# Seam between two layers: the post-norm's second product and both sums of squares move to GpSimd

## The chip, the cores and the metric

The kernel runs on one core of one Trainium2 chip. The metric is the device time of one execution in microseconds (us). A core has a matrix engine (TensorE, PE in the profile; its weight loads are PEld), a vector engine (VectorE, DVE), an activation engine (ScalarE, ACT), a programmable vector engine (GpSimd, POOL) and a sequencer that only issues transfers here (SyncE, SP). Each engine runs its own instructions strictly in their written order; semaphores make an instruction wait for one on another engine. SBUF is the on-chip working memory of 128 partitions, PSUM the small memory into which TensorE writes.

## The reference

Two equal layers (`DEPTH = 2`) on `x` of 512 tokens by 1024 features, float32. Each layer normalises `x`, makes one wide projection, runs a gated linear recurrence (8 heads) and a sliding-window attention (16 heads) on parts of it, gates both, and projects back:

```python
def rms_norm(x, g):
    y = xf * lax.rsqrt(jnp.mean(xf * xf, axis=-1, keepdims=True) + NORM_EPS)
    return (y * g.astype(jnp.float32)).astype(x.dtype)

def hybrid_layer(x, w_in, w_out, g_pre, g_post, lb, g_head, sinks):
    h = rms_norm(x, g_pre)
    proj = jnp.einsum('bsd,de->bse', h, w_in)
    ...
    y = jnp.einsum('bse,ed->bsd', jnp.concatenate([o_h, o_a], axis=-1), w_out)
    return x + rms_norm(y, g_post)
```

What matters here is the end of one layer and the start of the next: `x + rms_norm(y, g_post)`, then `rms_norm(., g_pre)` of the next layer, on 1024 features per token.

## The kernel before

**Tiles.** The 512 tokens are four tiles of 128 (`tt` 0 to 3, one token per partition). The 1024 features of a tile are two halves of 512 (`ch` or `c`, 0 and 1), since one PSUM bank holds 128x512 float32. Every matrix product is float32 made of three products of a high and a low part; weights and activations are split into `whi`/`wlo` and `hhi`/`hlo` by a cast on ScalarE (L178, L401) and a subtraction on VectorE (L179, L405).

**The stream of matrix products.** All projections of both layers stand in one queue of units. A unit accumulates one 128x512 (or 128x256) result in one of three PSUM banks `pj` (L284) and has an evacuation that runs when it is done. The last units of layer 0 are the eight of the out projection's last part (four tiles by two halves); the next are the key and value units of layer 1 (`wkv`, four tiles, 128x256), which need the new normalised and transposed activations `hhi`, `hlo` tile by tile; after them come the query units of layer 1, which need all four tiles.

**The seam.** For each tile, `final` and `pre_norm` do this, in this order of dependence:

- L850 (VectorE): adds the unit's result out of PSUM to `y`, per half.
- L892 (ScalarE): square of the half of `y`, with the row's sum into a column of `ss`.
- L894 (GpSimd): `y` of half 0 times the post-norm's weight `gpost`, in place. L899 (VectorE): the same for half 1, into `yg` (shown as tile `s`).
- `rstd2`: L343 (VectorE) adds the two sums of squares and epsilon, one number per row; L345 (GpSimd) raises it to the power -1/2: `r`.
- L906 (VectorE), per half: `x` plus the product times `r`, which is the layer's output (tile `a`); a transfer stores it.
- `pre_norm`: L377 (ScalarE) squares each half of `a` with its sum, `rstd2` again (L343, L345), L392 (VectorE) scales each half with the row's factor and the next weight, which lies in PSUM (`xn`).
- `rest`: L397 (TensorE) transposes four blocks of a half of `xn` into one of three PSUM banks `sc`, L401 (ScalarE) makes `hhi`, L405 (VectorE) `hlo` of it.

**What sets the order.** The code is written in the order of the stream of units; a scheduler then orders each engine's instructions by that order and by when it reckons their inputs ready, except where `pin` keeps the written order (the transposes L397 are pinned). So the order of the seam's instructions on VectorE and ScalarE depends on the engines that the program names.

Of the kernel before, what the change touches and what calls it, by code (L numbers as in the profile page):

```python
# [10 lines left out]
F32 = mybir.dt.float32  # L11
# [3 lines left out]
ALU = mybir.AluOpType  # L15
# [10 lines left out]
EPS = 1e-6  # L26
# [43 lines left out]
def hybrid_kernel(ctx: ExitStack, tc: tile.TileContext, x, wkv, win, wout, g_pre, g_post, lbp, ghead, sinks,  # L70
                  gcol_c, cos_f, sin_f, cos_t, sin_t, masks_c, out):
    nc = tc.nc
    P = 128
# [5 lines left out]
    sm = ctx.enter_context(tc.tile_pool(name="sm", bufs=4))  # L79
# [16 lines left out]
    def ac():  # L96
        return ps.tile([P, 512], F32, tag="ac", name="ac", bufs=8 - PJ - SC)

    def tmp(tag, dt=F32, n=1):

        t = tp.tile([P, n, 512] if n > 1 else [P, 512], dt, tag=tag, name=tag, bufs=TB[tag])
        return t
# [96 lines left out]
    def later(steps, key, fn):  # L199

        waiting.append([steps, key, fn])
# [138 lines left out]
    def rstd2(ss, keep=lambda ins: ins):  # L340

        t = sm.tile([P, 1], F32, tag="s1", name="s1")
        keep(nc.vector.scalar_tensor_tensor(t, ss[:, 0:1], EPS, ss[:, 1:2], op0=ALU.add, op1=ALU.add))  # L343
        r = sm.tile([P, 1], F32, tag="r1", name="r1")
        keep(nc.gpsimd.tensor_tensor(r, t, mhalf[:, 0:1], op=ALU.pow))  # L345
        return r

    def halves(tag):
        t = tmp(tag, n=2)
        return [t[:, 0], t[:, 1]]  # L350

    def load_g(g):
        t = halves("b")
        for c in range(2):
            nc.sync.dma_start(t[c], g[c * 512:(c + 1) * 512].partition_broadcast(P))
        return t
# [57 lines left out]
    def pre_norm(tt, xt, g, hT, key, defer):  # L414
        m = Norm(tt, xt, g, hT)
        m.square(0)
        m.square(1)
        m.r = rstd2(m.ss)
        m.scale(0)
        m.scale(1)  # L420
        later(defer, None, lambda: m.rest(0))
        later(defer, key, lambda: m.rest(1))

    def new_hT():
        return (hp.tile([P, KT, SEQ], F32R, tag="hhi", name="hhi"), hp.tile([P, KT, SEQ], F32R, tag="hlo", name="hlo"))


    def layer(l, last):
# [243 lines left out]
        def hgrn(a):  # L672
# [3 lines left out]
            for j, f, k, q, A in hs:  # L676
                f2, k2, q2 = (blocks(t, 2) for t in (f, k, q))
                qb, kb = halves("b")
                qb2, kb2 = blocks(qb, 2), blocks(kb, 2)
                re = halves("a")[0][:, 0:256]  # L680
                nc.vector.reciprocal(re, f2[:, :, 1])  # L681
                nc.scalar.copy(qb2[:, :, 0], q2[:, :, 0])
                nc.vector.tensor_tensor(qb2[:, :, 1], q2[:, :, 1], f2[:, :, 1], op=ALU.mult)
                nc.scalar.copy(kb2[:, :, 0], k2[:, :, 0])
                nc.vector.tensor_tensor(kb2[:, :, 1], k2[:, :, 1], re, op=ALU.mult)
                qbs.append(qb)
                kbs.append(kb)

                nc.gpsimd.tensor_tensor(k2[:, :, 0], k2[:, :, 0], f2[:, :, 1], op=ALU.mult)
                nc.vector.tensor_tensor(q2, qb2, f2[:, :, 0].unsqueeze(2).broadcast_to([P, SEQ // 2, 2]), op=ALU.mult)  # L690
                nc.vector.tensor_tensor(f2[:, :, 0], f2[:, :, 0], f2[:, :, 1], op=ALU.mult)
                tots.append(f2[:, :, 0])
                yield 3.5
# [174 lines left out]
        hT2 = {}  # L868

        def final(tt, ch, c0, n):  # L870
            split = n < 512
            if ch == 0:
                if tt == 0:
                    hT2["gpost"] = load_g(g_post[l])
                    if not last:
                        hT2["gpre"] = [ac() for _ in range(2)]
                        for c, t in enumerate(load_g(g_pre[l + 1])):
                            nc.scalar.copy(hT2["gpre"][c], t)
                        state["limit"] = slab_first["in", l + 1, QA][0] + 2
                        hT[l + 1] = new_hT()  # L880
                hT2["x"] = halves("a")
                for c in range(2):
                    nc.sync.dma_start(hT2["x"][c], (x if l == 0 else x_mid)[tt * P:(tt + 1) * P, c * 512:(c + 1) * 512])
                hT2["ss"] = sm.tile([P, 2], F32, tag="ss", name="ss")
            xt, ss, y = hT2["x"], hT2["ss"], yt[tt]
            if c0:

                hT2["ss"] = sm.tile([P, 2], F32, tag="ss", name="ss")
                nc.vector.tensor_tensor(hT2["ss"][:, 0:1], ss[:, 0:1], ss[:, 1:2], op=ALU.add)
                ss = hT2["ss"]  # L890
            junk = tmp("u")
            nc.scalar.activation(junk[:, 0:n], y[:, ch, c0:c0 + n], AF.Square, scale=1.0 / 32.0, accum_out=ss[:, ch:ch + 1])  # L892
            if ch == 0:
                nc.gpsimd.tensor_tensor(y[:, 0], y[:, 0], hT2["gpost"][0], op=ALU.mult)  # L894
                return
            if not c0:
                hT2["yg"] = tmp("s")
            yg = hT2["yg"]
            nc.vector.tensor_tensor(yg[:, c0:c0 + n], y[:, 1, c0:c0 + n], hT2["gpost"][1][:, c0:c0 + n], op=ALU.mult)  # L899
            if split and not c0:  # L900
                return
            r = rstd2(ss)
            parts = [(0, y[:, 0], 0, 512)] + [(1, yg, e, n) for e in range(0, 512, n)]
            for i, (c, v, e, w) in enumerate(parts):
                xs = xt[c][:, e:e + w]
                nc.vector.scalar_tensor_tensor(xs, v[:, e:e + w], r, xs, op0=ALU.mult, op1=ALU.add)  # L906
                (nc.scalar if split and i == 1 else nc.sync).dma_start(
                    (out if last else x_mid)[tt * P:(tt + 1) * P, c * 512 + e:c * 512 + e + w], xs)
            if not last:
                pre_norm(tt, xt, hT2["gpre"], hT[l + 1], ("h", l + 1, tt), DEFER)  # L910
# [48 lines left out]
    mhalf = const.tile([P, 4], F32, name="mhalf")  # L959
# [23 lines left out]
    m, n = head[0], head[1]  # L983
# [146 lines left out]
```

## Time and profile before

| | |
|---|---|
| median of 3 runs (lowest, highest) | 927.55 us (927.0, 927.8) |
| the profiled execution: its time, its span | 927.92 us, 926.2 us |
| granted TensorE clock, mean | 0.999 |
| busy: PE, DVE, ACT, POOL | 908.4, 672.1, 462.5, 268.8 us |
| the seam, from the first L894 to the first query unit of layer 1 | 444.7 to 480.65 us of the span |

A row of a timeline gives the start in us from the span's beginning, the duration in us, the engine, the line, the operation, output<-inputs by the program's names, the shape, and in brackets the idle time of the engine before it and what ended it. Consecutive alike instructions are merged (x2, x8). A row of a group by tile gives minimum, median and maximum in ns, then first and last start. A row of waits gives the total in us, how often, and the longest. A row of windows gives the length and the busy time of each engine, with the instructions counted, in that stretch.

### The profile page before, as it was taken

The numbers are of one execution on the slowest core, as the hardware profiler recorded it, in microseconds if no ns is written. First come the engines' busy times: TensorE is split into PE (matmuls) and PEld (weight loads), VectorE is DVE, ScalarE is ACT, GpSimd is POOL, SyncE is SP. The second block draws the span as 40 slices with busy tenths as digits, with TensorE's granted clock in tenths as the row PEclk, the third lists the DMA queues.
The fourth block names the chain that finished last, engine by engine and source line by source line (L and its number), as shares of the span: only waits on it lengthen the run. The fifth ranks groups of instructions, "written<-read, shape, count | busy, mean of one in ns | idle before, by whom it ended". The sixth has DMA issues, their size and how long they took to land.

```text
span 926.2 us, 18985 instructions
## 1 busy us (share of the span) xinstructions
PE 908.4 (98%) x7240; PEld 751.1 (81%) x7240; DVE 672.1 (73%) x1326; ACT 462.5 (50%) x1100; POOL 268.8 (29%) x286
## 2 busy tenths in 40 slices
PE   8999999999999999999989999999999999999996
PEld 6888887878888888788878878888787887888885
DVE  5968977885766783955786689878867577748556
ACT  5535767536364451444453466674554636325242
POOL 3425443242221311311332254441323203113102
PEclk9999999999999999999999999999999999999999
DMA  6684612322222242423356555122223223323213
GB/s 223 187 234 135 171 36 80 92 82 80 70 86 94 64 136 69 138 70 112 117 160 178 162 148 171 58 69 92 70 80 99 62 81 114 104 70 94 91 35 136
DMA packets 56570, 100.74 MB, mean 109 GB/s; under 512 B 6560, under 2 KB 9120, under 8 KB 56480
## 3 DMA queue, kind: packets, MB, share of 16 engines
q1 hardware_dynamic: 56192, 99.40, 35.8%
q8 instruction: 57, 0.93, 0.4%
q14 instruction: 33, 0.27, 0.1%
q10 hardware_dynamic: 288, 0.14, 0.1%
HBM read 86.93 MB, written 12.58 MB: 107 GB/s over the span
## 4 chain that ended last, share of the span: by engine, by line
PE 85%; DVE 8%; ACT 3%; issue 2%; POOL 1%; DMA 0%; POOLq 0%; DVEq 0%; SPq 0%; ACTq 0%
PE pj L284 71%; PE sc L713 2%; PE sc L552 2%; PE ac L605 2%; DVE wlo L179 2%; PE ac L782 2%; PE ac L785 1%; PE ac L770 1%; ACT s L566 1%; PE sc L579 1%; PE sc L830 1%; DVE mx L557 1%; POOL r L345 1%; DVE a L331 1%; PE sc L760 1%
## 5 line engine op out<-in xcount | busy, mean ns | idle before, releaser
L284 PE MATMUL pj<-hhi,wlo 128*128 128x512 f32 x512 | 205.3, 401 | 0.0
L179 DVE TENSOR_TENSOR wlo<-raw,whi 128x512 fp32r<-128x512 f32 x249 | 182.5, 746 | 27.1 <-ACT whi L178 26.2
L284 PE MATMUL pj<-hhi,whi 128*128 128x512 f32 x512 | 200.0, 391 | 0.0
L284 PE MATMUL pj<-hlo,whi 128*128 128x512 f32 x512 | 199.7, 390 | 0.0
L178 ACT CAST whi<-raw 128x512 fp32r<-128x512 f32 x256 | 155.0, 621 | 84.1 <-PE pj L284 71.5
L284 PE MATMUL pj<-whi,ops 128*128 128x512 f32 (+1 forms) x520 | 173.5, 395 | 0.0
L284 PEld LDWEIGHTS pj<-whi,ops 128*128 128x128 f32 x520 | 97.2, 188 | 19.6
L284 PEld LDWEIGHTS pj<-hhi,whi 128*128 128x128 f32 x512 | 96.1, 188 | 20.9
L284 PEld LDWEIGHTS pj<-hhi,wlo 128*128 128x128 f32 x512 | 96.2, 188 | 19.2
L284 PEld LDWEIGHTS pj<-hlo,whi 128*128 128x128 f32 x512 | 96.3, 188 | 18.3
L284 PE MATMUL pj<-whi,hlo 128*128 128x512 f32 x256 | 103.5, 405 | 0.0
L284 PE MATMUL pj<-wlo,hhi 128*128 128x512 f32 x256 | 100.4, 392 | 0.3 <-DVE wlo L179 0.2
L284 PE MATMUL pj<-wlo,ops 128*128 128x512 f32 (+1 forms) x260 | 100.5, 387 | 0.0
L284 PE MATMUL pj<-whi,hhi 128*128 128x512 f32 x256 | 100.3, 392 | 0.0
L731 POOL TENSOR_TENSOR k<-k,tot 128x256 f32<-128x256 f32 x80 | 64.9, 830 | 108.7 <-PE sc L713 61.2
L566 ACT ACTIVATE s<-sc,negm 128x128 f32<-128x128 f32 x128 | 45.5, 368 | 38.6 <-DVE negm L560 38.6
L730 DVE TENSOR_TENSOR q<-q,tot 128x256 f32<-128x256 f32 x80 | 51.3, 673 | 14.5 <-PE sc L713 9.5
L284 PEld LDWEIGHTS pj<-whi,hhi 128*128 128x128 f32 x256 | 48.1, 188 | 10.2
L284 PEld LDWEIGHTS pj<-wlo,ops 128*128 128x128 f32 x260 | 49.0, 188 | 8.7
L284 PEld LDWEIGHTS pj<-wlo,hhi 128*128 128x128 f32 x256 | 48.3, 189 | 8.9 <-DVE wlo L179 1.0
L284 PEld LDWEIGHTS pj<-whi,hlo 128*128 128x128 f32 x256 | 48.2, 188 | 8.0
L681 DVE RECIPROCAL a<-f 128x256 f32<-128x256 f32 x16 | 28.0, 1750 | 28.4 <-ACT f L658 26.1
(185 smaller groups left out, 1423.8 us busy)
## 6 DMA issues: line engine op xcount, KB each, us to landing
raw<-in_win_dram SPq DMA_DIRECT2D x192, 256.0 KB, 2.7
raw<-in_wout_dram SPq DMA_DIRECT2D x64, 256.0 KB, 2.7
stack<-rot SPq DMA_DIRECT2D x16, 512.0 KB, 3.5
qs<-stack SPq DMA_DIRECT2D x32, 256.0 KB, 4.5
a<-in_x_dram SPq DMA_DIRECT2D x12, 256.0 KB, 3.2
raw<-in_wkv_dram SPq DMA_DIRECT2D x8, 256.0 KB, 3.6
x_mid<-a SPq DMA_DIRECT2D x8, 256.0 KB, 2.2
a<-x_mid SPq DMA_DIRECT2D x8, 256.0 KB, 3.1
```

Source lines behind the costliest of these rows:

```text
L178: keep(nc.scalar.copy(hi, v))
L179: keep((nc.gpsimd if i in on_pool and i % 2 else nc.vector).tensor_tensor(lo, v, hi.bitcast(F32), op=ALU.subtract))
L284: nc.tensor.matmul(u.o, lhsT=u.sta(k, u.w)[i], rhs=u.mov(k, u.w)[j], start=(n == 0), stop=(n == len(u.list) - 1))
L331: nc.vector.tensor_tensor(lo, src, hi.bitcast(F32), op=ALU.subtract)
L552: pin(nc.tensor.matmul(S[:, h * 256:(h + 1) * 256], lhsT=q[:, 2 * hp_ + h, t_], rhs=kst[v][p][:, (n - 1) * P:(n + 1) * P], start=(h == 0 a ...
L566: nc.scalar.activation(pt[:, h * P:(h + 1) * P], cur[h], AF.Exp, bias=negm[:, h:h + 1], scale=SCALE, accum_out=sums[:, h:h + 1])
L605: pin(nc.tensor.matmul(U, lhsT=vst[v][:, blk, :], rhs=d, start=(i == 0), stop=(i == len(terms) - 1)))
L681: nc.vector.reciprocal(re, f2[:, :, 1])
L713: pin(nc.tensor.matmul(L[32 * b:32 * b + 32, c:c + 16], lhsT=k[:, o_:o_ + 32], rhs=qv[:, blk:blk + qu, 1, :], start=True, stop=True, tile_ ...
L730: nc.vector.tensor_tensor(qv[:, :, 1, :], qv[:, :, 1, :], tv[:, :, 0].unsqueeze(2).broadcast_to([P, nb, hh]), op=ALU.mult)
L731: nc.gpsimd.tensor_tensor(kv_[:, :, 0, :], kv_[:, :, 0, :], tv[:, :, 1].unsqueeze(2).broadcast_to([P, nb, hh]), op=ALU.mult)
L782: pin(nc.tensor.matmul(O[:, c], lhsT=A[:, c], rhs=vs(j, n), start=(n == 0), stop=False))
```

## The change

```diff
+    def sum_power(ss, keep=lambda ins: ins):
+        t = sm.tile([P, 1], F32, tag="s1", name="s1")
+        keep(nc.gpsimd.tensor_tensor(t, ss[:, 0:1], ss[:, 1:2], op=ALU.add))
+        r = sm.tile([P, 1], F32, tag="r1", name="r1")
+        keep(nc.gpsimd.tensor_tensor(r, t, mhalf[:, 0:1], op=ALU.pow))
+        return r
+
+    def add_eps(ss):
+        nc.gpsimd.tensor_scalar(ss[:, 0:1], ss[:, 0:1], EPS, None, op0=ALU.add)
...
     def pre_norm(tt, xt, g, hT, key, defer):
         m = Norm(tt, xt, g, hT)
         m.square(0)
+        add_eps(m.ss)
         m.square(1)
-        m.r = rstd2(m.ss)
+        m.r = sum_power(m.ss)
...
             if ch == 0:
                 nc.gpsimd.tensor_tensor(y[:, 0], y[:, 0], hT2["gpost"][0], op=ALU.mult)
+                if not last:
+                    add_eps(ss)
                 return
...
-            nc.vector.tensor_tensor(yg[:, c0:c0 + n], y[:, 1, c0:c0 + n], hT2["gpost"][1][:, c0:c0 + n], op=ALU.mult)
+            eng = nc.vector if last else nc.gpsimd
+            eng.tensor_tensor(yg[:, c0:c0 + n], y[:, 1, c0:c0 + n], hT2["gpost"][1][:, c0:c0 + n], op=ALU.mult)
...
-            r = rstd2(ss)
+            r = rstd2(ss) if last else sum_power(ss)
```

At the end of layer 0 alone, the product of half 1 (four of 128x512) goes from VectorE to GpSimd. The eight instructions that add two sums of squares and epsilon (L343) become sixteen on GpSimd: epsilon is added to the first sum as soon as that is there (`add_eps`), and the second sum is added in front of the power (`sum_power`). The end of layer 1 and the start of the program stay as they were. Line numbers in the changed program are: L357 `add_eps`, L351 and L353 the two of `sum_power`, L906 the product of half 0 and L914 that of half 1 on GpSimd, L862 the evacuation (L850 before), L921 the output (L906 before), L403 the scaling (L392 before), L416 the low part (L405 before).

On VectorE at the seam, tiles 0 and 1 (`y_2755` and `y_2770` are the `y` of tiles 0 and 1, `a_5166` the output of tile 0, `xn_5205` and `xn_5206` the scaled tile 0). Before:

```order
L850 TENSOR_TENSOR y_2755<-pj_5146,y_2755 128x512
L899 TENSOR_TENSOR s_5195<-y_2755,b_5154 128x512
L343 SCALAR_TENSOR_TENSOR s1_5197<-ss_5169 128x1
L906 SCALAR_TENSOR_TENSOR a_5166<-y_2755,r1_5199,a_5166 128x512
L850 TENSOR_TENSOR y_2770<-pj_5176,y_2770 128x512
L906 SCALAR_TENSOR_TENSOR a_5166<-s_5195,r1_5199,a_5166 128x512
L343 SCALAR_TENSOR_TENSOR s1_5209<-ss_5206 128x1
L850 TENSOR_TENSOR y_2770<-pj_5218,y_2770 128x512
L392 SCALAR_TENSOR_TENSOR xn_5205<-a_5166,r1_5211,ac_5157 128x512
L392 SCALAR_TENSOR_TENSOR xn_5205<-a_5166,r1_5211,ac_5158 128x512
L899 TENSOR_TENSOR s_5252<-y_2770,b_5154 128x512
L343 SCALAR_TENSOR_TENSOR s1_5254<-ss_5232 128x1
```

And with the change:

```order
L862 TENSOR_TENSOR y_2755<-pj_5146,y_2755 128x512
L921 SCALAR_TENSOR_TENSOR a_5166<-y_2755,r1_5200,a_5166 128x512
L862 TENSOR_TENSOR y_2770<-pj_5177,y_2770 128x512
L921 SCALAR_TENSOR_TENSOR a_5166<-s_5196,r1_5200,a_5166 128x512
L403 SCALAR_TENSOR_TENSOR xn_5206<-a_5166,r1_5213,ac_5157 128x512
L862 TENSOR_TENSOR y_2770<-pj_5220,y_2770 128x512
L403 SCALAR_TENSOR_TENSOR xn_5206<-a_5166,r1_5213,ac_5158 128x512
L921 SCALAR_TENSOR_TENSOR a_5231<-y_2770,r1_5259,a_5231 128x512
```

The evacuation of half 1 of tile 1 (`pj_5218` before, `pj_5220` now) stood ahead of both scalings of tile 0 and now stands behind the first of them.

On GpSimd at the same place (`r1_5199`, `r1_5200` are the post-norm's factor of tile 0, `r1_5211`, `r1_5213` the pre-norm's factor of tile 0, `r1_5256`, `r1_5259` the post-norm's of tile 1). Before:

```order
L894 TENSOR_TENSOR y_2755<-y_2755,b_5154 128x512
L345 TENSOR_TENSOR r1_5199<-s1_5197,mhalf_107 128x1
L894 TENSOR_TENSOR y_2770<-y_2770,b_5154 128x512
L345 TENSOR_TENSOR r1_5211<-s1_5209,mhalf_107 128x1
L345 TENSOR_TENSOR r1_5256<-s1_5254,mhalf_107 128x1
```

With the change:

```order
L914 TENSOR_TENSOR s_5196<-y_2755,b_5154 128x512
L351 TENSOR_TENSOR s1_5198<-ss_5169 128x1
L353 TENSOR_TENSOR r1_5200<-s1_5198,mhalf_107 128x1
L357 TENSOR_SCALAR ss_5207<-ss_5207 128x1
L906 TENSOR_TENSOR y_2770<-y_2770,b_5154 128x512
L357 TENSOR_SCALAR ss_5234<-ss_5234 128x1
L351 TENSOR_TENSOR s1_5211<-ss_5207 128x1
L353 TENSOR_TENSOR r1_5213<-s1_5211,mhalf_107 128x1
L914 TENSOR_TENSOR s_5255<-y_2770,b_5154 128x512
L351 TENSOR_TENSOR s1_5257<-ss_5234 128x1
L353 TENSOR_TENSOR r1_5259<-s1_5257,mhalf_107 128x1
```

Each factor now has the product of half 1, or an addition of epsilon and the sum, ahead of it on GpSimd itself.

On VectorE further on, at tiles 2 and 3 (`y_2828` is the `y` of tile 3, `xn_5319` and `xn_5324` the scaled tile 2, `a_5355` and `a_5361` the output of tile 3, `hlo_5165<-sc0_78` and `<-sc1_79` the low part of tile 1). Before:

```order
L850 TENSOR_TENSOR y_2828<-pj_5332,y_2828 128x512
L343 SCALAR_TENSOR_TENSOR s1_5323<-ss_5320 128x1
L179 TENSOR_TENSOR wlo_5476<-raw_5045,whi_5475 128x512
L392 SCALAR_TENSOR_TENSOR xn_5319<-a_5286,r1_5325,ac_5157 128x512
L392 SCALAR_TENSOR_TENSOR xn_5319<-a_5286,r1_5325,ac_5158 128x512
L899 TENSOR_TENSOR s_5374<-y_2828,b_5154 128x512
L343 SCALAR_TENSOR_TENSOR s1_5376<-ss_5358 128x1
L405 TENSOR_TENSOR hlo_5165<-sc0_78,hhi_5164 128x4x128
L906 SCALAR_TENSOR_TENSOR a_5355<-y_2828,r1_5378,a_5355 128x512
```

With the change:

```order
L403 SCALAR_TENSOR_TENSOR xn_5324<-a_5290,r1_5331,ac_5157 128x512
L862 TENSOR_TENSOR y_2828<-pj_5338,y_2828 128x512
L403 SCALAR_TENSOR_TENSOR xn_5324<-a_5290,r1_5331,ac_5158 128x512
L416 TENSOR_TENSOR hlo_5165<-sc2_80,hhi_5164 128x4x128
L921 SCALAR_TENSOR_TENSOR a_5361<-y_2828,r1_5385,a_5361 128x512
L921 SCALAR_TENSOR_TENSOR a_5361<-s_5381,r1_5385,a_5361 128x512
L416 TENSOR_TENSOR hlo_5165<-sc0_78,hhi_5164 128x4x128
L416 TENSOR_TENSOR hlo_5165<-sc1_79,hhi_5164 128x4x128
```

The evacuation of the last half (`pj_5332` before, `pj_5338` now) again stands behind a scaling, and the first low part of tile 1 (`sc0_78`) stands behind both outputs of tile 3 instead of ahead of them.

On TensorE the two transposes of tile 3, which had three products between them, now follow each other; transfers on SP keep their order.

## The prediction

> **What bounds the kernel now.** First the page: its span, its engines and the chain that ended last.
>
> ```profile
> span 926.2 us, 18985 instructions
> PE 908.4 (98%) x7240; PEld 751.1 (81%) x7240; DVE 672.1 (73%) x1326; ACT 462.5 (50%) x1100; POOL 268.8 (29%) x286
> PE 85%; DVE 8%; ACT 3%; issue 2%; POOL 1%; DMA 0%; POOLq 0%; DVEq 0%; SPq 0%; ACTq 0%
> ```
>
> TensorE is busy for 98% of the span and carries 85% of the chain. A change elsewhere gains or loses only what TensorE waits less or more. So I looked next at TensorE's waits in the stretch that holds the seam (440 to 490 us), and at the busy time of the engines in four stretches of 7 us:
>
> ```profile
> PE pj L284 <- ACT hhi L401: 1.0, 1, 1.0
> PE sc L397 <- DVE hlo L405: 1.0, 1, 1.0
> PE sc L397 <- DVE xn L392: 0.7, 1, 0.7
> PE pj L284 <- DVE hlo L405: 0.2, 1, 0.2
> 455.00:462.00 7.00, 7.00 (x37) 5.87 (x36) 5.75 (x10) 4.04 (x11) 2.75 (x3) 1.00 0.44 152
> 462.00:469.00 7.00, 5.96 (x48) 5.64 (x47) 6.45 (x13) 3.96 (x11) 2.69 (x3) 1.00 0.55 173
> 469.00:476.00 7.00, 5.15 (x40) 4.47 (x39) 6.07 (x11) 3.15 (x8) 1.08 (x2) 1.00 0.48 164
> ```
>
> TensorE loses 1.0 + 1.0 + 0.7 + 0.2 = 2.9 us at the seam, all after 462 us, when the out projection's products are used up and each tile's transposes and key products come straight out of the norms. That is all that a relief could win. VectorE is busy for 6.45 of 7 us there, GpSimd for 2.7: this speaks for moving work, until one asks in which order the work is released. The timelines of VectorE, ScalarE and GpSimd show it for tiles 0 and 1 (the last rows are the starts for tiles 2 and 3):
>
> ```profile
> 449.29 0.75 DVE L906 SCALAR_TENSOR_TENSOR a<-y,r,a 128x512 f32<-128x512 f32 x1 [0.66 <-POOL r L345]
> 450.56 0.74 DVE L906 SCALAR_TENSOR_TENSOR a<-s,r,a 128x512 f32<-128x512 f32 x1
> 451.27 0.19 ACT L892 ACTIVATION_READ_ACCUMULATOR u<-y 128x1 f32 x1
> 451.54 1.29 POOL L894 TENSOR_TENSOR y<-y,b 128x512 f32<-128x512 f32 x1 [2.28 <-ACT u L892]
> 451.89 0.19 ACT L377 ACTIVATION_READ_ACCUMULATOR hlo<-a 128x1 f32 x1
> 452.11 0.74 DVE L343 SCALAR_TENSOR_TENSOR s<-ss 128x1 f32<-128x1 f32 x1 [0.81 <-ACT hlo L377]
> 452.92 0.55 POOL L345 TENSOR_TENSOR r<-s,mhalf 128x1 f32<-128x1 f32 x1
> 453.51 1.40 DVE L392 SCALAR_TENSOR_TENSOR xn<-a,r,ac 128x512 f32<-128x512 f32 x2
> 454.84 0.68 DVE L899 TENSOR_TENSOR s<-y,b 128x512 f32<-128x512 f32 x1
> 455.44 0.15 DVE L343 SCALAR_TENSOR_TENSOR s<-ss 128x1 f32<-128x1 f32 x1
> 455.67 0.54 POOL L345 TENSOR_TENSOR r<-s,mhalf 128x1 f32<-128x1 f32 x1 [2.19 <-DVE s L343]
> 456.24 0.75 DVE L906 SCALAR_TENSOR_TENSOR a<-y,r,a 128x512 f32<-128x512 f32 x1
> 462.98 0.75 DVE L906 SCALAR_TENSOR_TENSOR a<-y,r,a 128x512 f32<-128x512 f32 x1
> 470.38 0.75 DVE L906 SCALAR_TENSOR_TENSOR a<-y,r,a 128x512 f32<-128x512 f32 x1
> ```
>
> The seam is a loop: output of a tile, its squares, its sum, its power, its scaling, then the next tile's product and sum, its power, its output. Each round starts from the scaling of the one before. The outputs start at 449.29, 456.24, 462.98 and 470.38: rounds of 6.95, 6.74 and 7.40 us. Whatever lengthens a step of the round counts again for each tile. Note the sum L343 at 452.11: one number per row, yet 0.74 us against 0.15 at 455.44. It ends at 452.85, just after the product L894 on GpSimd (451.54 + 1.29 = 452.83). A VectorE instruction with both inputs in SBUF is held until a product on GpSimd ends.
>
> **The change, part by part.** The prices, from groups by tile:
>
> ```profile
> L894 POOL TENSOR_TENSOR y<-y,b x4: 1287/1290/1296, 444.7 to 465.2; 128x512 f32<-128x512 f32 x4
> L899 DVE TENSOR_TENSOR s<-y,b x4: 679/686/691, 447.7 to 468.9; 128x512 f32<-128x512 f32 x4
> L382 POOL TENSOR_SCALAR s<-ss x2: 221/366/510, 10.0 to 15.9; 128x1 f32<-128x1 f32 x2
> L335 POOL TENSOR_SCALAR hr<-hss x16: 193/193/562, 223.4 to 871.7; 128x4 f32<-128x4 f32 x16
> ```
>
> Removed from VectorE are four products of 0.60 us of its queue and eight sums of 0.07 to 0.66. *Product:* four go from 0.69 us on VectorE to 1.29 on GpSimd; I take L894's time, same shape and operands. *Epsilon:* like L382 unhindered, 0.21 (0.19 to 0.22). *Sum of two columns on GpSimd:* no row has it. From below it is bounded by L335, the cheapest small instruction there (0.19), from above by the power on two inputs of the same shape (0.54, L345 at 455.67), which does the same reading and writing and more arithmetic. I take 0.22, near the lower end, since an addition is nearer to L382 than to a power. Below nothing is excluded: each is an instruction more in GpSimd's queue.
>
> The Trainium skill, GPSIMD Engine Reference, section "Performance versus the Vector engine", gives 2.6 cycles per element at 1.2 GHz and 4497 ns for 2048 elements, of which 2048 x 2.6 / 1.2 = 4437 ns are elements: a fixed part of about 0.06 us as an estimate. With 0.06 for each epsilon and each sum the loss below would be about 2.2 us instead of 3.6. The trace disagrees for the nearest thing it has, 193 ns for four elements, and I keep the row.
>
> Now the new order, carried through with these durations. VectorE's next instruction of 512 starts 0.60 (from PSUM) or 0.66 us (L906, L392) after the last; a signal to GpSimd takes 0.08, back 0.03. Carrying the order of before through like this, with the hold above, puts the first query product at 480.38; the trace has 480.65 (last fence of this part).
>
> *First output.* The half-1 product starts at 447.69, when `y` is there, and ends at 448.99; sum 449.18, signal, power 449.80, output 449.83. Before 449.29: **+0.54**. Before, VectorE's product ran beside ScalarE's square; now the sum stands behind the product in one queue.
>
> *Round 0 to 1.* From the output at 449.83 the squares end 2.84 later, at 452.67 (before: 452.08, 2.79 later). GpSimd is then in the product of tile 1's half 0, which waited for L892's sum (2.17 after the output, as at 451.46 before) and is ahead in its queue: 452.08 to 453.37. Then epsilon of tile 1 (453.55), the sum (453.74), the power (454.36). That is 4.53 after the output, where L345 ended 4.18 after it before (453.47): +0.35. The first scaling at 454.40; behind it in VectorE's queue the evacuation of half 1, which waited there for the power, 455.06 to 455.75; only then the product on GpSimd, 455.83 to 457.12. From the power's end to the product's start 1.47 against 1.37 (454.84 less 453.47): +0.10. The product takes 1.29 where the next step followed L899 after 0.60: +0.69. Sum, signal and power 0.81 against 0.77 (455.44 to 456.21): +0.04. Output at 457.96, round 8.13: **+1.18**.
>
> *Round 1 to 2.* The same steps: squares end 460.80, half-0 product 460.21 to 461.50, power 462.49, evacuation to 463.88, product 463.96 to 465.25. Here VectorE starts a weight's low part L179, now earlier in its queue, and the two hold each other. What that costs is seen later in the trace:
>
> ```profile
> 477.88 1.37 POOL L179 TENSOR_TENSOR wlo<-raw,whi 128x512 fp32r<-128x512 f32 x1 [4.02 <-ACT whi L178]
> 478.89 0.91 DVE L179 TENSOR_TENSOR wlo<-raw,whi 128x512 fp32r<-128x512 f32 x1 [0.80 <-ACT whi L178]
> 459.67 0.68 DVE L899 TENSOR_TENSOR s<-y,b 128x512 f32<-128x512 f32 x1
> 459.83 0.92 POOL L345 TENSOR_TENSOR r<-s,mhalf 128x1 f32<-128x1 f32 x1
> ```
>
> VectorE ends 0.55 after GpSimd (479.80 against 479.25), and a small GpSimd instruction ends late behind a VectorE product (0.92 instead of 0.54). So L179 ends at 465.79, the sum at 465.87 instead of 465.47, the power at 466.49, the output starts at 466.53: 8.57 against 6.74, **+1.83**. The old round was the shorter since L899 was done ahead of the scaling.
>
> *Round 2 to 3.* Both outputs stand together (466.53, 467.20), squares end 468.70, and this power is ahead of the half-0 product: 469.62. Scaling 469.66, evacuation 470.32 to 471.01, product to 472.38, sum 472.57, power 473.19, output 473.22: 6.69 against 7.40, **-0.71**; the old order had an evacuation and a low part between the outputs.
>
> Together 0.54 + 1.18 + 1.83 - 0.71 = +2.84 for the output of tile 3 (473.22 against 470.38).
>
> *The end.* TensorE's rows, and from the page the time in which a tile of `x` lands:
>
> ```profile
> 458.30 1.03 PE L397 MATMUL sc<-ident,xn 128*128 128x128 f32 x8
> 459.09 0.47 PE L284 MATMUL pj<-whi,ops 128*128 128x512 f32 x1
> 467.54 1.35 PE L284 MATMUL pj<-wkv,hhi 128*128 128x256 f32 x9 [1.04 <-ACT hhi L401]
> 470.32 0.65 PE L397 MATMUL sc<-ident,xn 128*128 128x128 f32 x4 [1.00 <-DVE hlo L405]
> 477.77 2.08 PE L284 MATMUL pj<-wkv,hhi 128*128 128x256 f32 x16
> 479.69 1.12 PE L284 MATMUL pj<-wkv,hlo 128*128 128x256 f32 x8
> 480.65 0.40 PE L284 MATMUL pj<-hhi,wlo 128*128 128x512 f32 x1
> ...
> a<-in_x_dram SPq DMA_DIRECT2D x12, 256.0 KB, 3.2
> ```
>
> The first low part of tile 1 now waits behind both outputs of tile 3: it starts at 473.22 + 1.33 = 474.55, and the bank that it frees lets the second transposes of tile 2 start at 475.29. Before, these waited for the same bank at 470.32. From there TensorE has 63 key products of 0.12 us (16 in 1.92, 477.77 to 479.69) and twelve transposes (eight in 0.79): 7.56 + 1.2, and 0.2 for restarts, and by my times no wait: 484.25 for the first query product, against 480.65: **+3.6 us**. TensorE, its waits included, then stands still longer in earlier places too: about 2.4 us for `hhi` of tile 1 at 465, 2.5 for a bank at 469, 1.4 for `hlo`.
>
> Hidden at no cost: the relief of VectorE (it waits for powers instead), the epsilon of half 0 of `y` (ready before the second square is; 0.21 a tile if not), and the transfers of `x` (tile 3's is released by the second scaling of tile 1, 464.5, and lands 3.2 later, 5 us before it is needed). Stores and weight transfers keep their order behind these on SP's queue. Behind the seam everything is counted from the first query product, so the delay is carried to the end. The profiled execution lies 0.37 us above the median and 1.7 above its span: 927.92 + 3.6 = 931.5, by the median 927.55 + 3.6 = **931.2 us**.
>
> **The rivals.**
> - *The sum is dear.* If an addition on GpSimd costs like a power, 0.54 us, the same carrying-through gives +6.0 us: 933.6. For it: it has two inputs as L345 has. Against: L382.
> - *The delay counts once.* If TensorE's stock of products hides all rounds but the last, what is left is the first power's +0.54 and one product's +0.69: 928.8, no change by the measure below. For it: TensorE has no wait before 467.5 us. Against: each round starts from the scaling of the round before.
> - *VectorE is the bound, and its relief wins.* The place is 462 to 476 us, where it is busy for 12.5 of 14. If the factors come before VectorE asks for them, the 2.9 us of waiting go: 924.7, faster. It decides from the point where a round on GpSimd is shorter than VectorE's own work of a round. Against: VectorE keeps per tile eight instructions of 0.60 to 0.66, about 5.1 us, less than any round here, so it isn't what the rounds wait for.
>
> That the change does not do what it says is excluded: the order on GpSimd shows every moved instruction.
>
> **How the numbers follow.** Forecast 0.62 (930.3 to 932.3), sum dear 0.15, counts once 0.12, relief 0.07, something slower still 0.04. A measurement tells a difference of 0.2% (1.9 us) from none. Slower: 0.62 + 0.15 + 0.04 = 0.81; same 0.12; faster 0.07. The range goes from 928.7, which takes in the single delay, to 934.0, which takes in the dear sum; outside lie the relief and the rest.
>
> **What would show it.** Right: four products of 1.29 us at L914 on GpSimd, outputs L921 8.1 and 8.6 us apart for tiles 0 to 2, then 6.7; VectorE idle in front of L921 and L403 for GpSimd's power; TensorE's longest waits at the seam 2.4 and 2.5 us; the first query product near 484.2. Wrong: rounds of 7 us or less, which would mean that the power is not what ends them; L351 far from 0.22 us, which moves the sum by 0.7 us per 0.1 (it stands on the path seven times); or a seam that is 3.6 us longer with an unchanged total.

## The result and the profile after

The changed kernel takes 931.86 us (median of 5 runs, 931.76 to 932.46), the kernel before 927.32 us on the same chip (5 runs, 927.0 to 927.8): a ratio of 1.0048, 95% interval 1.0034 to 1.0061. It is slower, by 4.5 us. The profiled execution took 931.76 us. The page of the changed kernel:

```profile
span 930.0 us, 18995 instructions
PE 908.8 (98%) x7240; PEld 751.0 (81%) x7240; DVE 667.7 (72%) x1314; ACT 462.9 (50%) x1100; POOL 276.8 (30%) x306
```

TensorE does the same work as before (908.8 us against 908.4), VectorE 4.4 us less, and the span is 3.8 us longer. So the loss is waiting. TensorE's waits between 440 and 490 us, of the changed kernel:

```profile
PE sc L408 <- DVE hlo L416: 3.0, 2, 2.2
PE pj L284 <- ACT hhi L412: 2.3, 1, 2.3
PE pj L284 <- DVE hlo L416: 1.2, 1, 1.2
PE pj L284 <- DVE y L862: 0.3, 1, 0.3
```

6.8 us against 2.9: this is most of the loss. The start of the program ran some 0.5 us shorter in this execution, so times from the span's beginning can't be set side by side. I count from the last transposes of `z`, which TensorE does shortly ahead of the seam, to the first query product behind it, and call this the seam. TensorE's rows of before, then of the changed kernel:

```profile
444.91 0.60 PE L830 MATMUL sc<-ident,z 128*128 128x128 f32 x4
```
```profile
444.44 0.60 PE L842 MATMUL sc<-ident,z 128*128 128x128 f32 x4
465.19 1.35 PE L284 MATMUL pj<-wkv,hhi 128*128 128x256 f32 x9 [2.26 <-ACT hhi L412]
469.13 0.66 PE L408 MATMUL sc<-ident,xn 128*128 128x128 f32 x4 [2.15 <-DVE hlo L416]
472.31 0.74 PE L284 MATMUL pj<-wkv,hlo 128*128 128x256 f32 x4 [1.21 <-DVE hlo L416]
475.42 0.66 PE L408 MATMUL sc<-ident,xn 128*128 128x128 f32 x4 [0.86 <-DVE hlo L416]
484.33 0.40 PE L284 MATMUL pj<-hhi,wlo 128*128 128x512 f32 x1
```

Before: 480.65 - 444.91 = 35.74 us. After: 484.33 - 444.44 = 39.89 us, **+4.15 us**, inside the interval of the medians (3.2 to 5.7 us). Behind the first query product both take the same time to the end of the span, 445.6 and 445.7 us. The loss lies in the seam. There, VectorE and GpSimd of the changed kernel in one row of time (tiles 0 and 1, then the outputs of tiles 2 and 3):

```profile
449.37 0.75 DVE L921 SCALAR_TENSOR_TENSOR a<-y,r,a 128x512 f32<-128x512 f32 x1 [2.22 <-POOL r L353]
451.62 1.29 POOL L906 TENSOR_TENSOR y<-y,b 128x512 f32<-128x512 f32 x1 [0.17 <-ACT u L904]
452.99 0.21 POOL L357 TENSOR_SCALAR ss<-ss 128x1 f32<-128x1 f32 x1
453.27 0.19 POOL L351 TENSOR_TENSOR s<-ss 128x1 f32<-128x1 f32 x1
453.55 0.58 POOL L353 TENSOR_TENSOR r<-s,mhalf 128x1 f32<-128x1 f32 x1
454.16 0.75 DVE L403 SCALAR_TENSOR_TENSOR xn<-a,r,ac 128x512 f32<-128x512 f32 x1 [2.78 <-POOL r L353]
454.83 0.68 DVE L862 TENSOR_TENSOR y<-pj,y 128x512 f32<-128x512 f32 x1
455.59 1.29 POOL L914 TENSOR_TENSOR s<-y,b 128x512 f32<-128x512 f32 x1 [1.47 <-DVE y L862]
456.83 0.20 POOL L351 TENSOR_TENSOR s<-ss 128x1 f32<-128x1 f32 x1
457.11 0.55 POOL L353 TENSOR_TENSOR r<-s,mhalf 128x1 f32<-128x1 f32 x1
457.70 0.75 DVE L921 SCALAR_TENSOR_TENSOR a<-y,r,a 128x512 f32<-128x512 f32 x1 [1.53 <-POOL r L353]
466.46 0.75 DVE L921 SCALAR_TENSOR_TENSOR a<-y,r,a 128x512 f32<-128x512 f32 x1 [0.71 <-POOL r L353]
473.35 0.75 DVE L921 SCALAR_TENSOR_TENSOR a<-y,r,a 128x512 f32<-128x512 f32 x1 [1.10 <-POOL r L353]
```

Read it as one thread: output, GpSimd's product of the next tile, epsilon, sum, power, scaling, evacuation, the other product, sum, power, output. VectorE stands idle for 2.78 us in front of the scaling and 1.53 us in front of the output, each time for GpSimd's power. The outputs are 8.33, 8.76 and 6.89 us apart; before it was 6.95, 6.74 and 7.40. The busy time in two stretches of the changed kernel (columns PE, PEld, DVE, ACT, POOL):

```profile
462.00:469.00 7.00, 2.71 (x18) 1.98 (x16) 5.79 (x8) 3.43 (x9) 3.30 (x6) 1.00 0.39 127
469.00:476.00 7.00, 4.80 (x37) 4.36 (x38) 5.29 (x9) 3.86 (x12) 4.51 (x9) 1.00 0.37 119
```

VectorE is busy for less (5.79 and 5.29 us of 7, where it had 6.45 and 6.07), and TensorE for less still (2.71 and 4.80, where it had 5.96 and 5.15).

### The profile page after: what moved, and what is told of

Same layout as the page of the kernel before. It is cut to its first block, busy times and chain, and to the rows that moved or that the text cites. A ratio compares the mean times of both kernels' runs of the same rounds, so it can differ in the third digit from the quotient of the medians.

```text
span 930.0 us, 18995 instructions
## 1 busy us (share of the span) xinstructions
PE 908.8 (98%) x7240; PEld 751.0 (81%) x7240; DVE 667.7 (72%) x1314; ACT 462.9 (50%) x1100; POOL 276.8 (30%) x306
## 4 chain that ended last, share of the span: by engine, by line
PE 85%; DVE 7%; ACT 3%; POOL 2%; issue 2%; DMA 0%; POOLq 0%; DVEq 0%; ACTq 0%
PE pj L284 71%; PE sc L725 2%; PE sc L564 2%; PE ac L617 2%; DVE wlo L179 2%; PE ac L794 2%; PE ac L797 1%; PE ac L782 1%; ACT s L578 1%; PE sc L591 1%; PE sc L842 1%; DVE mx L569 1%; DVE a L331 1%; PE sc L772 1%; DVE a L921 1%
## 5 line engine op out<-in xcount | busy, mean ns | idle before, releaser
L179 DVE TENSOR_TENSOR wlo<-raw,whi 128x512 fp32r<-128x512 f32 x249 | 183.2, 749 | 27.3 <-ACT whi L178 26.3
L743 POOL TENSOR_TENSOR k<-k,f 128x256 f32<-128x256 f32 x16 | 14.8, 945 | 113.4 <-PE sc L725 113.4
```

The lines of the kernel that those rows point to most:

```text
L179: keep((nc.gpsimd if i in on_pool and i % 2 else nc.vector).tensor_tensor(lo, v, hi.bitcast(F32), op=ALU.subtract))
L743: nc.gpsimd.tensor_tensor(kv_[:, :, 0, :], kv_[:, :, 0, :], tv[:, :, 1].unsqueeze(2).broadcast_to([P, nb, hh]), op=ALU.mult)
```

## The experiments

All times are of the profiled execution of each kernel, counted from the last transposes of `z` to the first query product; "rounds" are the distances of the first outputs of tiles 0 to 3. The medians stand against the kernel before on the same chip (928.02 us for the second to fifth row; 927.59 for the next four; 927.88 for the last but one and 927.32 for the last), the interval of each ratio being about 0.09 to 0.13% (0.8 to 1.2 us) to either side, so that the seam in the trace says more of a small step than the total does. It is one execution of each kernel, but rounds that an edit leaves alone repeat to 0.01 us (the rows of tile 3 and of tile 0). V is VectorE, G GpSimd.

| kernel | half 0, half 1, sums | seam, us | against before | first output | rounds | median against before |
|---|---|---|---|---|---|---|
| before | G V V | 35.74 | | 4.38 | 6.95, 6.74, 7.40 | |
| product only | G G V | 37.53 | +1.79 | 4.76 | 6.35, 8.26, 7.48 | +1.2 |
| sums only | G V G | 37.23 | +1.49 | 4.55 | 8.11, 6.74, 6.85 | +1.2 |
| product of tile 3 only | G V V, tile 3 G G V | 36.79 | +1.05 | 4.39 | 6.95, 6.74, 8.04 | +1.1 |
| both products on VectorE | V V V | 33.03 | -2.71 | 4.38 | 6.38, 6.56, 6.51 | -3.1 |
| product of tile 0 only | G V V, tile 0 G G V | 36.12 | +0.38 | 4.76 | 6.96, 6.74, 7.39 | +0.9 |
| sums on GpSimd, products on VectorE | V V G | 35.33 | -0.41 | 4.55 | 7.25, 5.85, 6.91 | 0.0 |
| products swapped | V G V | 36.64 | +0.90 | 4.76 | 5.77, 7.71, 7.73 | +1.7 |
| both on VectorE, late scaling | V V V | 33.32 | -2.42 | 4.38 | 6.24, 4.77, 7.68 | -2.7 |
| the change, half 0 on VectorE | V G G | 38.74 | +3.00 | 4.93 | 7.48, 7.91, 7.18 | +2.8 |
| the change | G G G | 39.89 | +4.15 | 4.93 | 8.33, 8.76, 6.89 | +4.5 |

The theory is that of the prediction: the seam is a loop over the tiles, and a step that gets longer costs where it is the late one. The expectations' "carrying the order through" is the prediction's method, with the durations that the trace of the changed kernel gave. An edit changes two things at once: the engine of a step, and the order in which the scheduler then puts the other steps on VectorE. No run holds that order fixed, so each price below is that of both together.

**The two halves of the change apart.** First the product alone, against the kernel before:

```diff
-            nc.vector.tensor_tensor(yg[...], y[:, 1, ...], gpost, op=ALU.mult)
+            eng = nc.vector if last else nc.gpsimd
+            eng.tensor_tensor(yg[...], y[:, 1, ...], gpost, op=ALU.mult)
```

> Half 1's product on GpSimd as in the change, the sums and epsilons as before (one VectorE instruction). The seam is measured from the last transposes of z (444.91 us before, 444.44 after) to the first query product (480.65, 484.33): 35.74 us before, 39.89 after. The loop theory (a step that gets longer is paid in each round in which it is the late one): carrying the order through with the measured durations gives outputs at 449.7, 456.1, 464.4 and 471.9 and a seam of 37.5 us, +1.8, so about 929.1 us. Rival 'the relief of VectorE counts': four products of 0.60 us leave its queue, up to -2.4, 924.9. Rival 'the delay counts once': +0.7, 928.0. Rival 'the sums do it': +0, 927.3.

Measured: seam 37.53 us, +1.79; median 929.25 us, ratio 1.0016 (1.0007 to 1.0025). The relief of VectorE falls, and so do "the delay counts once" (+0.7) and "the sums do it" (+0). The rounds show more than the sum: 6.35 us for the first, shorter than before, then 8.26. GpSimd and VectorE of the kernel with the product alone:

```profile
453.63 0.55 POOL L345 TENSOR_TENSOR r<-s,mhalf 128x1 f32<-128x1 f32 x1
454.23 1.30 POOL L911 TENSOR_TENSOR s<-y,b 128x512 f32<-128x512 f32 x1
459.97 0.54 POOL L345 TENSOR_TENSOR r<-s,mhalf 128x1 f32<-128x1 f32 x1
461.97 1.29 POOL L911 TENSOR_TENSOR s<-y,b 128x512 f32<-128x512 f32 x1 [1.46 <-DVE y L861]
```
```profile
453.47 0.68 DVE L861 TENSOR_TENSOR y<-pj,y 128x512 f32<-128x512 f32 x1
454.21 1.41 DVE L403 SCALAR_TENSOR_TENSOR xn<-a,r,ac 128x512 f32<-128x512 f32 x2
460.54 0.75 DVE L403 SCALAR_TENSOR_TENSOR xn<-a,r,ac 128x512 f32<-128x512 f32 x1 [0.66 <-POOL r L345]
461.21 0.68 DVE L861 TENSOR_TENSOR y<-pj,y 128x512 f32<-128x512 f32 x1
462.47 1.34 DVE L179 TENSOR_TENSOR wlo<-raw,whi 128x512 fp32r<-128x512 f32 x1
463.73 0.15 DVE L343 SCALAR_TENSOR_TENSOR s<-ss 128x1 f32<-128x1 f32 x1
```

For tile 1 the evacuation L861 (453.47) stands ahead of the scaling: the product starts 0.05 us after the power and runs beside the scalings. For tile 2 it stands behind the first scaling (461.21), and the product starts 1.46 us after the power. The same product is free in one round and costs in the next. Two things differ: the place of one VectorE instruction, and the weight's low part L179 that VectorE began beside the product of tile 2. It took 1.34 us, and the sum behind it started 0.47 us after the product's end (463.26). In the changed kernel the evacuation stands behind the first scaling in every round.

Then the sums alone:

```diff
+        add_eps(m.ss)
...
-        m.r = rstd2(m.ss)
+        m.r = sum_power(m.ss)
...
+                if not last:
+                    add_eps(ss)
...
-            r = rstd2(ss)
+            r = rstd2(ss) if last else sum_power(ss)
```

> Epsilon and sum on GpSimd as in the change, half 1's product on VectorE as before. Loop theory: seam 36.4 us, +0.7, about 928.0 us; with the product-only kernel's +1.8 this makes 2.5 of the 4.15 that the whole change costs, and the rest comes from both standing in the same queue. Rival 'the sums do it': +4 or so, 931.3. Rival 'the parts add up': the whole change's 4.15 less whatever the product alone costs. Rival 'the relief counts': eight sums of VectorE's queue, 0.07 to 0.66 each, are gone: -0.5 to -1, 926.5.

Measured: seam 37.23 us, +1.49, twice the expected 0.7; median 929.25 us, ratio 1.0015 (1.0006 to 1.0024). The relief falls, and so does "the sums do it". Most of the miss, 0.48 of 0.79 us, is in one power (VectorE, then GpSimd, of this kernel):

```profile
470.14 0.68 DVE L913 TENSOR_TENSOR s<-y,b 128x512 f32<-128x512 f32 x1
```
```profile
470.21 1.04 POOL L353 TENSOR_TENSOR r<-s,mhalf 128x1 f32<-128x1 f32 x1
```

It started 0.07 us after a VectorE product and took 1.04 us instead of the median of 0.565: 0.48 us. When the sum stood on VectorE it stood behind that product in the same queue, and the power started after both. The two halves cost 1.79 + 1.49 = 3.28 us apart and 4.15 together, 0.87 more, so in the traces they do not simply add up.

**Does the delay count once?** The product on GpSimd for one tile only, the last or the first:

```diff
-            eng = nc.vector if last else nc.gpsimd
+            eng = nc.vector if last or tt != 3 else nc.gpsimd
```

> As the product-only kernel, but only the last tile's product goes to GpSimd; the other three stay on VectorE. Loop theory: the last round's delay has no slack behind it: +1.0 us, seam 36.7, about 928.3 us. Rival 'the delay counts once': this one kernel costs all that the four products cost together (+1.8 by the theory's price, or whatever the product-only kernel shows). Rival 'the relief counts': -0.6 at most, 926.7.

> As the product-only kernel, but only the first tile's product goes to GpSimd. Measured so far, as the seam from the last transposes of z to the first query product (35.74 us before): product-only +1.79, product of the last tile alone +1.05. Loop theory: the first output comes 0.4 us later and all later ones with it, so the delay is neither lost nor multiplied: +0.4, seam 36.2, about 0.4 us above the kernel before. Rival 'the delay counts once, at the last round': an early delay is swallowed by the products that TensorE still has in stock: 0. Rival 'each round pays again': four times the first round's 0.4, +1.6.

Measured: the last tile's +1.05 (rounds unchanged up to the last, which is 8.04 instead of 7.40), the first tile's +0.38 (first output 0.38 later, all rounds unchanged to 0.01). Medians: ratio 1.0014 (1.0005 to 1.0023) and 1.0009 (1.0000 to 1.0018); the second can't be told from no change by the total, but its trace is clear. An early delay isn't swallowed, against the rival "the delay counts once"; and it isn't multiplied either. What costs in each round is that each round has its own late step. Of the last tile's 1.05 us, 0.64 is in its round. The other 0.41 lies behind the output: there VectorE does one low part ahead of tile 3's scalings where it did two before, and TensorE waits 0.60 us (at 476.28) for the next.

The last tile's product did not take 1.29 us there (VectorE, then GpSimd, of the kernel with tile 3's product alone):

```profile
466.58 0.68 DVE L179 TENSOR_TENSOR wlo<-raw,whi 128x512 fp32r<-128x512 f32 x1
```
```profile
466.60 1.80 POOL L911 TENSOR_TENSOR s<-y,b 128x512 f32<-128x512 f32 x1
```

It was held by a weight's low part that VectorE had begun 0.02 us earlier.

**The opposite of the change.** Half 0's product, which the kernel before has on GpSimd, goes to VectorE too, so that VectorE has four products more:

```diff
-                nc.gpsimd.tensor_tensor(y[:, 0], y[:, 0], hT2["gpost"][0], op=ALU.mult)
+                (nc.gpsimd if last else nc.vector).tensor_tensor(y[:, 0], y[:, 0], hT2["gpost"][0], op=ALU.mult)
```

> The opposite of the change: from before, half 0's product of the seam is put on VectorE too, so that no product of the seam is on GpSimd; sums and powers as before. Loop theory: the products take 0.69 instead of 1.29 us, no sum is held by a GpSimd product and no power stands behind one: outputs at 449.2, 455.7, 462.4 and 468.9, seam 33.1 us, -2.6, so about 924.7 us, faster than both. Rival 'VectorE's work is what ends it': four more products of 0.60 us in its queue, +2.4, 929.7. Rival 'the delay counts once': one round's gain, -0.6, 926.7.

Measured: seam 33.03 us, -2.71; median 924.89 us, ratio 0.9972 (0.9960 to 0.9983): faster than the kernel before and than the changed one, as the loop theory said. TensorE's waits and the windows of this kernel:

```profile
PE sc L397 <- DVE hlo L405: 0.7, 1, 0.7
```
```profile
462.00:469.00 7.00, 6.35 (x54) 6.08 (x53) 6.45 (x13) 4.48 (x12) 1.40 (x2) 1.00 0.39 145
469.00:476.00 7.00, 6.95 (x58) 6.70 (x57) 6.59 (x11) 4.85 (x12) 0.91 (x2) 1.00 0.59 187
```

VectorE is busier than ever (6.59 us of 7), and of the 2.9 us of TensorE's waiting 0.7 are left. VectorE's busy share was no bound. Part of it was not work either. The page of this kernel:

```profile
PE 907.7 (98%) x7240; PEld 751.1 (81%) x7240; DVE 674.0 (73%) x1330; ACT 463.2 (50%) x1100; POOL 263.9 (29%) x282
```

Four products of 0.69 us more are 2.8 us, and VectorE is busy for only 1.9 us more (674.0 against 672.1). The sums show why: before, three of the seam's eight took 0.74 (the one in the prediction's third fence), 0.74 (at 459.01) and 0.44 us (at 466.11), each ending 0.02 us behind a GpSimd product, and here all eight take 0.15 or 0.16. So some 1.5 us of VectorE's busy time before was its instructions being held. (The totals hold other differences too, so they need not agree with this to the tenth.)

**The order once more.** The same, with the two scalings of a tile written out behind the following evacuations, to see whether the better order of the scalings gives more:

```diff
-        m.scale(0)
-        m.scale(1)
+        later(9, None, lambda: (m.scale(0), m.scale(1)))
```

> Both products of the seam on VectorE, sums as before, and the pre-norm's two scalings are written out after the following evacuations instead of at once, so that in VectorE's order the second scaling of a tile stands behind the next tile's product and sum. Seam of the kernel with both products on VectorE: 33.03 us, with 0.7 us of TensorE's waiting left at the seam. Loop theory: the order of the scalings now matters little, as no round waits for GpSimd's product any more: outputs at 449.2, 455.6, 460.4 and 468.2, seam 32.8, -0.3 against that kernel and about -2.9 us against before. Rival 'the scalings are what is late for the transposes': moving them back costs, seam above 33.5.

Measured: seam 33.32 us, 0.29 longer than without this step, where 32.8 was expected; median 924.86 us (0.9970, 0.9960 to 0.9981), the same total. Tile 3's output begins 0.76 us earlier (4.38 + 6.24 + 4.77 + 7.68 = 23.07 us after the anchor, against 23.83), but its second half only 0.21 us, and a scaling of tile 2 stands behind it (VectorE of this kernel):

```profile
468.83 0.75 DVE L905 SCALAR_TENSOR_TENSOR a<-s,r,a 128x512 f32<-128x512 f32 x1 [0.47 <-DMA a<-in_x_dram]
469.50 0.74 DVE L392 SCALAR_TENSOR_TENSOR xn<-a,r,ac 128x512 f32<-128x512 f32 x1
```

VectorE waits in the first row for the transfer of `x` of tile 3, which goes out behind the second scaling of tile 1. The step put that scaling off, and the transfer was issued 20.00 us after the anchor instead of 16.21. TensorE then waits 0.38 us for the scaling in the second row. So the step delayed a transfer besides what it was meant to do, and whether a faster loop could win the 0.7 us that TensorE still waits in both kernels is not shown.

**Work or place?** The two products change places, half 0's to VectorE and half 1's to GpSimd, so that each engine does as many instructions of the same shapes as before:

```diff
-                nc.gpsimd.tensor_tensor(y[:, 0], y[:, 0], ...)
+                (nc.gpsimd if last else nc.vector).tensor_tensor(y[:, 0], y[:, 0], ...)
...
-            nc.vector.tensor_tensor(yg[...], y[:, 1, ...], ...)
+            (nc.vector if last else nc.gpsimd).tensor_tensor(yg[...], y[:, 1, ...], ...)
```

> From before, the two products of each tile change places: half 0's on VectorE, half 1's on GpSimd; each engine does as many instructions of the same shapes as before. Loop theory (what counts is where in the round the slow one stands: half 1 is evacuated last, and its product stands right before the output, half 0's has time): carrying the order through gives outputs at 449.7, 455.6, 463.3 and 471.1 and +1.0, seam 36.7. Rival 'the engines' work is what counts' (a bound by busy time, of VectorE or GpSimd): the same time as before, seam 35.7. Rival 'a GpSimd product costs wherever it stands': as before too, since there are as many; then product-only (+1.79, two a tile) and both on VectorE (-2.71, none) would be a straight line with this one at 0.

Measured: seam 36.64 us, +0.90; median 929.25 us, ratio 1.0018 (1.0009 to 1.0027). As many instructions of each kind on each engine, and slower: what counts is the place in the round and the order that follows from it, not how much each engine has to do. Half 0 of a tile is evacuated earlier (in the changed kernel at 450.04 us for tile 1, half 1 at 454.83), so its product has time; half 1's stands right ahead of the sum, the power and the output.

**Do the sums cost only behind GpSimd's products?** The change's sums, with both products on VectorE; against the changed kernel:

```diff
-                nc.gpsimd.tensor_tensor(y[:, 0], y[:, 0], ...)
+                (nc.gpsimd if last else nc.vector).tensor_tensor(y[:, 0], y[:, 0], ...)
...
-            eng = nc.vector if last else nc.gpsimd
-            eng.tensor_tensor(yg[...], y[:, 1, ...], ...)
+            nc.vector.tensor_tensor(yg[...], y[:, 1, ...], ...)
```

> Epsilon and sum on GpSimd as in the change, both products of the seam on VectorE, so that GpSimd has nothing but the small instructions. The kernel with both products on VectorE and the sums as before has a seam of 33.03 us (-2.71). Loop theory: even with GpSimd's queue empty a sum there costs 0.28 (0.20 and a gap of 0.08) where VectorE takes 0.15, and VectorE's products can hold the sums and powers; carrying the order through gives -0.7 against before, seam 35.0, so +1.9 for the sums. In the kernel with the sums alone the same sums cost +1.49. Rival 'the sums cost only because they stand behind the product in GpSimd's queue': no more than 4 rounds of 0.13, +0.5, seam 33.5. Rival 'the relief of VectorE counts': seam below 33.0.

Measured: seam 35.33 us, 2.30 longer than with the sums on VectorE; median 927.58 us against 927.59, ratio 1.0001 (0.9992 to 1.0010). So they cost as much with GpSimd's queue empty as behind its products (1.49 to 2.36 over the table), and the rival falls. A part of it is that GpSimd's small instructions now meet VectorE's products (VectorE, then GpSimd, of this kernel):

```profile
450.84 0.69 DVE L906 TENSOR_TENSOR y<-y,b 128x512 f32<-128x512 f32 x1 [0.19 <-ACT u L904]
```
```profile
450.89 0.71 POOL L357 TENSOR_SCALAR ss<-ss 128x1 f32<-128x1 f32 x1 [0.17 <-ACT u L904]
```

An epsilon takes 0.71 us. But the output of tile 3 comes only 0.73 us later than with the sums on VectorE (24.56 against 23.83 us after the anchor), and the seam is 2.30 longer. The rest lies in the low parts on VectorE, for which TensorE waits (the first low part of tile 0 with the sums on VectorE; then with the sums on GpSimd, and TensorE's waits there):

```profile
460.53 0.68 DVE L405 TENSOR_TENSOR hlo<-sc,hhi 128x512 fp32r<-128x512 f32 x1
```
```profile
463.67 0.69 DVE L416 TENSOR_TENSOR hlo<-sc,hhi 128x512 fp32r<-128x512 f32 x1
PE sc L408 <- DVE hlo L416: 1.4, 2, 0.9
PE pj L284 <- DVE hlo L416: 1.2, 1, 1.2
```

After the anchor these are 16.12 and 19.58 us: with the sums on VectorE this low part stands ahead of both outputs of tile 2, with the sums on GpSimd behind them. TensorE waits 2.6 us instead of 0.7. The order goes with the sums: the low part stands behind both outputs in all four kernels that have the sums on GpSimd, the change among them, and ahead of the first in before and in the five others that have them on VectorE. (The kernel with the late scaling is left out, since its order was written otherwise.) How much of the price of the sums is GpSimd's time and how much this order stays open.

**The last corner.** The change with half 0's product on VectorE (the first two lines of the diff above alone):

> The change with half 0's product put on VectorE: half 1's product, epsilons and sums on GpSimd. It is the missing corner of the table of three moves. Seams measured (last transposes of z to the first query product), half 0 / half 1 / sums by engine, V VectorE, G GpSimd: GVV 35.74 (before), GGV 37.53, VVV 33.03, VGV 36.64, GVG 37.23, GGG 39.89 (the change), VVG 35.33. Loop theory: epsilon, sum and power of the pre-norm no longer stand behind half 0's product in GpSimd's queue, but half 1's product still stands in every round: carrying the order through gives outputs at 449.8, 457.3, 465.2 and 473.0 and +3.3 against before, seam 39.0, 0.8 less than the change. Rival 'the costs of the moves add up': from VVV, half 1 costs 3.61 and the sums 2.30, so 38.9: no different here. Rival 'the product of half 0 in GpSimd's queue is what makes the change slow': near VVG, seam below 37.

Measured: seam 38.74 us, +3.00; median 930.7 us, ratio 1.0029 (1.0018 to 1.0041). The rival that half 0's product is what makes the change slow falls (a seam below 37). The loop theory (39.0) and "the costs add up" (38.9) can't be told apart here. The last round is counted to tile 3's first output, which is half 1's in this kernel; half 0's comes 0.67 us later. In this profile alone TensorE's granted clock fell in the seam, to 0.50 from 468 to 471 us, and seven key products took 1.84 us there (1.08 in the changed kernel); why it fell is not shown. TensorE then waits 0.97 us at 474.10 for a low part that stands behind tile 3's outputs (472.03 and 472.70), so by the trace that stretch did not set the end of the seam.

The table is now complete. Half 1's product on GpSimd costs 1.79 to 3.61 us whatever else stands there (37.53 - 35.74, 36.64 - 33.03, 39.89 - 37.23, 38.74 - 35.33), the sums 1.49 to 2.36, half 0's product 0.89 to 2.71: every move to GpSimd costs, in every company, each with the order that the scheduler makes of it.

## Why the prediction was right, point by point

- **The bound and the loop: right.** TensorE's work is unchanged, its waits went from 2.9 to 6.8 us, and the outputs carry the loss from tile to tile. The longest waits were foreseen as 2.4, 2.5 and 1.4 us for the right partners; they are 2.26, 2.15 and 1.21. The prediction took VectorE's new order as given, with the low parts behind the outputs, so it is right about engine and order together; it does not part them, and the runs do not either.
- **First output, +0.54: right.** 449.37 - 444.44 = 4.93 us after the anchor, 449.29 - 444.91 = 4.38 before: +0.55.
- **Rounds of 8.13, 8.57 and 6.69 us: the steps right, each 0.2 us too short** (8.33, 8.76, 6.89). The mis-sized term in the first two is the chain product, epsilon, sum, power on GpSimd. The prediction had 0.99 us from the product's end to the power's (453.37 to 454.36); it is 452.91 to 454.13, 1.22. The durations were near (0.21, 0.19 and 0.58 against 0.21, 0.22 and 0.54), but GpSimd leaves 0.08, 0.07 and 0.09 us between these instructions, where I had let them overlap by 0.03 and counted one signal of 0.08. In the third round it is chiefly the epsilon of tile 3, which I had taken as hidden:

```profile
470.94 0.22 POOL L357 TENSOR_SCALAR ss<-ss 128x1 f32<-128x1 f32 x1
471.24 1.28 POOL L914 TENSOR_TENSOR s<-y,b 128x512 f32<-128x512 f32 x1
```

  The evacuation for this product ended at 470.99; the product started 0.25 us after that, where a signal takes 0.08, behind the epsilon in GpSimd's queue. The 0.21 us that were named as the price without cover came due.
- **Output of tile 3, +2.84: it is +3.44** (28.91 against 25.47 after the anchor), the three times 0.2. **From there to the first query product +0.76 more: it is +0.71.** The sum was +3.6 and the seam has +4.15; the medians are 4.5 us apart.
- **The hold between L179 and the product: right.** The sum behind them took 0.64 us and the power started at 465.88; the groups by tile of the changed kernel show it as the maximum:

```profile
L351 POOL TENSOR_TENSOR s<-ss x8: 192/195/642, 448.5 to 475.7; 128x1 f32<-128x1 f32 x8
L914 POOL TENSOR_TENSOR s<-y,b x4: 1272/1285/1293, 447.2 to 471.2; 128x512 f32<-128x512 f32 x4
```

- **Prices: right.** The product 1.285 us (taken 1.29), the sum 0.195 (taken 0.22, near the lower end of 0.19 to 0.54). So the rival "the sum is dear" is out. The estimate from the Trainium skill's GPSIMD Engine Reference (section "Performance versus the Vector engine"), a fixed part of 0.06 us, is out as well: 0.195 for one element in each partition, as the row of 0.193 for four had it.
- **"The delay counts once": wrong, shown** by the kernels with one tile's product and by the rounds. **"VectorE is the bound": wrong, shown** by the kernel that gives it four products more and is 3.1 us faster.
- **What the prediction did not ask:** it priced the products at their 1.29 us, and in the new order it reckoned with a hold only at L179. The kernel before already paid for GpSimd's other product: without it the seam is 2.71 us shorter, and TensorE's waits fall from 2.9 to 0.7 us. Most of the 2.9 us was to be won, by the opposite move.

## What to carry to other kernels

Before moving work off a busy engine, follow one tile through the loop in time and ask which instruction ends each wait; try a step that stands right ahead of the wait's end on the engine that does it soonest, even if that engine is the busier one. Read the new order of every engine too: moving one instruction can put another one late. Where a tiny instruction takes 0.7 us in one place and 0.15 in another, look for one that holds it: its engine's busy time then counts another engine's work. Where two engines hold each other, as here, try both products on the faster one before giving the slower one more.

## What the runs showed of the hardware

- **The hold goes both ways, and tiny instructions are not spared.** On VectorE a sum of 0.15 us took 0.74 beside a GpSimd product. On GpSimd an epsilon of 0.21 us took 0.71 beside a VectorE product, a power of 0.565 took 1.04, a product of 1.29 took 1.80; they ended 0.07 us (451.60 against 451.53), 0.43 us (471.25 against 470.82) and 1.14 us (468.40 against 467.26) after the VectorE instruction. So most of a power's or a product's own time, and a third of an epsilon's, still lay ahead when the other had ended. The Trainium skill, SBUF — State Buffer, section "Who interferes with whom", says that a VectorE instruction with two inputs in SBUF contends with a GpSimd instruction that reads SBUF, and that the order of issue decides which of them blocks. The trace agrees: in each of these three the VectorE instruction had started first, by 0.05, 0.07 and 0.02 us.
- **GpSimd's tiny instructions cost more than they take.** An addition on 128x1 takes 0.195 us and an epsilon 0.21, and between such instructions in a row lie 0.07 to 0.09 us more (452.91 to 452.99, 453.20 to 453.27, 453.46 to 453.55). The same addition with its epsilon takes VectorE 0.15 us in one instruction.
